# First mixer of a two-block transformer kernel: head projections with tokens on partitions, head norms along the free axis, then transposes

## The chip, the cores and the metric

The kernel runs as one program on one core of a Trainium2 chip. The metric is the device time of one execution in microseconds: 2159.94 us before the change, the median of three runs (2159.58 to 2167.09). TensorE multiplies a stationary operand (loaded by a weight load, up to 128x128) by a moving operand (up to 512 columns) into PSUM, in which a bank holds 512 fp32 values on each of 128 partitions. VectorE (DVE), ScalarE (ACT) and GpSimd (POOL) work beside it, and SyncE (SP) issues the DMAs.

## The reference, cut to what matters

Two transformer blocks on 512 tokens of width 1024, in fp32. The change lies in the mixer of the first block, between its two feed-forward parts:

```python
u = rms_norm(h, g_mix) @ w_in                       # 1024 -> 1952
q_lat, kv_lat, k_rope, qd, kd, vd = split(u, [256, 128, 32, 512, 512, 512])
# latent attention: 8 heads
q  = (rms_norm(q_lat, g_q_lat) @ w_q_up).reshape(S, 8, 96)     # 64 plain + 32 rotated
kv = (rms_norm(kv_lat, g_kv_lat) @ w_kv_up).reshape(S, 8, 128) # 64 keys + 64 values
q_nope = rms_norm(q[..., :64], g_q[:64]);  q_rot = apply_rope(rms_norm(q[..., 64:], g_q[64:]), cos, sin)
k_nope = rms_norm(kv[..., :64], g_k[:64]); k_rot = apply_rope(rms_norm(k_rope, g_k[64:]), cos, sin)
# differential attention: 4 heads, each with 2 x 64 queries and keys and 128 values
q = rms_norm(qd.reshape(S, 4, 2, 64), g_q);  k = rms_norm(kd.reshape(S, 4, 2, 64), g_k)
a = softmax(q1 @ k1.T * scale + bias) - lam * softmax(q2 @ k2.T * scale + bias)
o = rms_norm(a @ v, g_sub) * (1 - lambda_init)
h = h + concat(o_mla, o_diff) @ w_out
```

`rms_norm(x, g)` is x times the reciprocal root of the mean square of x along the last axis (plus 1e-6), times g. It is taken here over the 64 or 32 values of one head and one token.

## The kernel before, in words

Activations lie transposed: features on partitions, 512 tokens along the free axis. An fp32 product is made of three fp32r matmuls (`mm3`, L399 to L401): each operand is split into a rounded part (hi, by ScalarE) and a rest (lo, by VectorE or GpSimd), and hi·hi, hi·lo and lo·hi are added in PSUM. A weight block of 512 KB comes by a DMA into `wraw` (three buffers, L374), is split by ScalarE (L376) and by VectorE (L379) or GpSimd (L383) into `whl` (three buffers), and is then the stationary operand of 24 matmuls of 512 columns.

In the mixer a *task* is one weight block and what is done with it. `proj` (L615) multiplies a block of 128 output features with all tokens into one bank; `evacuate` (L630) multiplies it on VectorE by the token norm, which lies along the free axis as a tile broadcast over the partitions (`bcast`: four TensorE transposes and a ScalarE copy). There are twelve such blocks for the four differential heads (a query, a key and a value block each), four for the latents and the rotated key, and 72 matmuls of the up-projections in four tasks `t_mla`.

Since a head's 64 values lie across partitions, its mean square is a product with a matrix of ones: `row_rstd` (L483 to L489) squares a tile on ScalarE and multiplies it with a two-column constant on TensorE, four fp32 matmuls of two columns a tile, each of which shows as two records. The reciprocal roots then have tokens on partitions; `pairs` (L460) spreads them on VectorE and `bc2` (L468) transposes them, four transposes a tile, so that one VectorE operation (L769, L861, L869) can multiply them in. Values are needed with tokens on partitions: `transposes` (L564, L565) turns each value tile by four transposes and a ScalarE copy.

A generator `attention` goes through the items d0 to d3 and m0 to m3: scores, softmax, the transposes of the weights (L1076), the product with the values (L812, L911). `merge` interleaves it with the stream of tasks in a fixed ratio (100:135 by costs that the code yields), and the list `TASKS1` sets the order of the tasks. `need` holds an item back until its task is done and a lag has passed. From this program order, raised priorities (`high_priority`) and estimated times a scheduler writes the fixed order of each engine's queue. `stream` loads the weight of the running task and that of the next.

Of the kernel before, what the change touches and what calls it, by code (L numbers as in the profile page):

```python
# [31 lines left out]
TASKS1 = "q1 k1 v1 v0 kv q2 k2 v2 ql0 ql1 rq q3 bq k3 ple0 rkv kr v3 wkv bkv m0 m1 ple1 m2 wo2 m3 wo3 wo0"  # L32
# [47 lines left out]
def layout(inp):  # L80
# [20 lines left out]
    cols = []  # L101
    for h in range(HD):
        cols += [oqd + h * P + ar(P), okd + h * P + ar(P), ovd + h * P + ar(P)]
    cols += [oq + ar(256), okv + ar(128), kr, krp, kr, krp]
    L["w_inA"] = _a(w_in, np.concatenate(cols))
# [9 lines left out]
    wq = _a(g["w_q_up"][0], np.concatenate(qcols))  # L115
    L["w_qup"] = np.ascontiguousarray(wq.reshape(2, 4, P, 256).transpose(0, 2, 1, 3).reshape(2, P, 1024))
# [32 lines left out]
    L["c_rt1"] = np.concatenate([c, ss, c, ss], axis=0)  # L149
# [87 lines left out]
class Prog:  # L237
# [329 lines left out]
    def block1(self):  # L567
# [18 lines left out]
        rtab = self.U("rtab")  # L586
        nc.sync.dma_start(rtab, I["c_rt1"])
# [26 lines left out]
        def proj(w, evac=None, src=None, kc=KC, o=0):  # L614
            ps = self.G()  # L615
            for k in range(kc):
                c = slice(o + k * P, o + k * P + P)
                x = (xs if src is None else src)[k]
                self.mm3(ps, w[:, 0, c], w[:, 1, c], x[:, 0, :], x[:, 1, :], k == 0, k == kc - 1)
                if k % 2:  # L620
                    yield 1.3
            if evac is None and "rb" not in L_:
                L_["first"] = ps
                return
            evacuate(ps, L_["rb"] if evac is None else evac)
# [14 lines left out]
        def t_first(w):  # L640
            yield from proj(w)
            L_["r"] = self.rstd(acc2, D, "mix")

        def t_second(w):
            ps, first = self.G(), L_.pop("first")
            self.gemm(ps, w, xs, KC)
            L_["rb"] = self.bcast(L_.pop("r"), "mix")
            evacuate(first, L_["rb"])
            Y_[0] = [L_["y"]]
            evacuate(ps, L_["rb"])  # L650
            Y_[0].append(L_["y"])
            stats(("qk", 0), [(y, 0) for y in Y_[0]])
            yield

        def t_q(w, h):
            yield from proj(w)
            Y_[h] = [L_["y"]]

        def t_k(w, h):
            yield from proj(w)  # L660
            Y_[h].append(L_["y"])
            stats(("qk", h), [(y, 0) for y in Y_[h]])
            yield 1.0

        def t_v(w, h):
            yield from proj(w)
            vd[h] = self.U("vd")
            self.transposes(vd[h], L_["y"])
            mark(("v", h), 1.0)
            yield 0.4  # L670
# [32 lines left out]
        def t_b(w, k):  # L703
            L_["rb" + k] = self.bcast(L_["r" + k], k)
            yield 0.4

        def t_mla(w, p):
            if p % 2 == 0:
                L_["wq"] = w
            ql = [L_["ql", 0], L_["ql", 1]]  # L710
            ys = []
            for e in range(2):
                yield from proj(L_["wq"], L_["rbq"], ql, 2, ((2 * p + e) % 4) * 256)
                ys.append(L_["y"])
            for o in (0, 512):
                yield from proj(L_["wkv"], L_["rbkv"], [L_["kvl"]], 1, o + p * P)
                ys.append(L_["y"])
            yield 1.3
            vd["m", p] = self.U("vm")
            self.transposes(vd["m", p], ys[3])  # L720
            Y_["m", p] = ys
            stats(("m", p), [(ys[0], 1), (ys[1], 2), (ys[2], 0)])
            for e in range(2):
                rr = slice(64 * (1 - e), 64 * (1 - e) + 64)
                nc.vector.tensor_tensor(ys[e][rr], ys[e][rr], rtab[rr], op=OP.mult)
            yield 2.0
# [35 lines left out]

        def diff_n(h):
            yield from need(("qk", h))
            r = L_["qk", h]
            es = [self.pairs(r, 4, o) for o in (0, 2)]
            for y, e, g, d, n in ((Y_[h][0], es[0], gd[:, h : h + 1], q_, "dq"), (Y_[h][1], es[1], self.g1[:, GDK : GDK + 1], k_, "dk")):
# [5 lines left out]
            del Y_[h]  # L773
# [31 lines left out]
        def diff_o(h):  # L805
# [3 lines left out]
            for j in range(4):  # L809
                at = self.U("at")  # L810
                self.cols(at, a, j)
                mm(po, vd[h][:, j * P : (j + 1) * P], at, start=j == 0, stop=j == 3)  # L812
# [25 lines left out]
        def mla_kr(_):  # L838
# [4 lines left out]
            nc.vector.tensor_tensor(t, t, rtab, op=OP.mult)  # L843
# [12 lines left out]
        def mla_n(p):  # L856
            yield from need(("m", p))
            ys, r = Y_.pop(("m", p)), L_["m", p]
            es = [self.pairs(r, 6, o) for o in (4, 0, 2)]
            kn = self.U("kn")  # L860
            nc.vector.scalar_tensor_tensor(kn, ys[2], self.g1[:, GMKN : GMKN + 1], self.bc2(es[0]), op0=OP.mult, op1=OP.mult)  # L861
            yield 0.4
            q_["m", p], k_["m", p] = [], []
# [1316 lines left out]
```

## Time and profile before

| | before |
|---|---|
| time, median of three runs | 2159.94 us |
| the profiled execution, own time | 2162.42 us |
| its span, first to last instruction | 2160.6 us |
| TensorE busy | 97% of the span |
| VectorE, ScalarE, GpSimd busy | 44%, 33%, 25% |
| mean granted TensorE clock | 0.989 |
| the first mixer | about 380 to 712 us of the span |

How to read it: a busy TensorE is a queue that always has a matmul in flight. The recorded length of a matmul contains the passage through the array, so consecutive matmuls overlap in the records, and what one costs is the distance between the starts of neighbours. A granted clock of 1.00 is 2.4 GHz, 0.50 is 1.2 GHz.

### The profile page before, as it was taken

Reading aid. Unit: us, or ns where it says so; the run is one execution under the profiler, and the core shown is the slowest. Engines: PE = TensorE matmul, PEld = TensorE weight load, DVE = VectorE, ACT = ScalarE, POOL = GpSimd, SP = SyncE. Lnnn points to the kernel's source line nnn. Section 1 sums busy time; section 2 is a strip of 40 time slices with the busy share of each in tenths; the row PEclk is TensorE's granted clock in tenths of the full one; section 3 lists DMA queues with packets and bytes.
Section 4 is the critical chain, followed back from the end, with each engine's and each line's share of the span. In section 5 each row is a group of like instructions: output and inputs, shape, how many; then the busy total and the mean of one; then the engine's idle time right before and its main releaser. Section 6 shows DMA issues by size and latency. Waiting matters only on the chain.

```text
span 2160.6 us, 25910 instructions
## 1 busy us (share of the span) xinstructions
PE 2101.9 (97%) x10233; PEld 1508.2 (70%) x10233; DVE 955.3 (44%) x1695; ACT 720.2 (33%) x1201; POOL 547.1 (25%) x449
## 2 busy tenths in 40 slices
PE   8999999999999999999998999999999999999997
PEld 6888888767676788888777777667887455544544
DVE  4323234466775432323476994553353232322322
ACT  4213224445554422322444667442231111111112
POOL 3323234323331532323443445111230000000000
PEclk9999999999899999999999999999999999999999
DMA  4332323311010233332422111012626899999993
GB/s 163 98 90 96 98 89 116 115 59 59 10 50 30 88 98 95 92 97 88 124 78 69 50 40 45 30 49 69 241 78 234 355 412 411 421 411 414 408 395 158
DMA packets 67838, 330.73 MB, mean 153 GB/s; under 512 B 7792, under 2 KB 8960, under 8 KB 43648
## 3 DMA queue, kind: packets, MB, share of 16 engines
q1 hardware_dynamic: 67136, 327.97, 41.5%
q8 instruction: 82, 1.34, 0.2%
q10 hardware_dynamic: 576, 1.05, 0.1%
q14 instruction: 44, 0.36, 0.0%
HBM read 326.90 MB, written 2.10 MB: 152 GB/s over the span
## 4 chain that ended last, share of the span: by engine, by line
PE 83%; DVE 7%; ACT 4%; issue 3%; POOL 2%; DMA 0%; SPq 0%; DVEq 0%; POOLq 0%; ACTq 0%
PE pss L1743 10%; PE psg L399 10%; PE psg L401 10%; PE psg L400 10%; PE psg L1743 8%; PE pss L399 4%; PE pss L401 4%; PE pss L400 4%; PE pst L400 4%; PE pst L399 4%; PE pst L401 4%; PE pst L1743 4%; PE pst L486 1%; ACT whl L376 1%; PE pst L1748 1%
## 5 line engine op out<-in xcount | busy, mean ns | idle before, releaser
L383 POOL TENSOR_TENSOR whl<-wraw,whl 128x512 fp32r<-128x512 f32 x228 | 306.3, 1364 | 606.8 <-ACT whl L376 375.3
L376 ACT ACTIVATE whl<-wraw 128x1024 fp32r<-128x1024 f32 (+1 forms) x227 | 237.3, 1046 | 627.0 <-PE psg L401 254.5
L379 DVE TENSOR_TENSOR whl<-wraw,whl 128x1024 fp32r<-128x1024 f32 (+1 forms) x113 | 157.2, 1391 | 60.7 <-ACT whl L376 60.5
L2043 POOL TENSOR_TENSOR fr<-fv,mhalf 128x1 f32<-128x1 f32 x4 | 2.2, 547 | 513.8 <-DVE fv L2042 512.1
L1743 PE MATMUL pss<-mw,xe 128*64 128x512 f32 x512 | 115.3, 592 | 0.0
L1743 PE MATMUL pss<-mw,hT 128*64 128x512 f32 x480 | 109.7, 611 | 0.5 <-ACT hT L1921 0.5
L524 POOL TENSOR_TENSOR t<-t,t 128x512 f32<-128x512 f32 x44 | 57.3, 1303 | 202.4 <-DVE t L523 196.9
L1743 PE MATMUL psg<-mw,xe 128*64 128x512 f32 x480 | 108.1, 592 | 0.0
L523 DVE TENSOR_TENSOR t<-pss,rb_f 128x512 f32<-128x512 f32 x44 | 30.4, 691 | 163.1 <-PE pss L401 163.1
L556 DVE SCALAR_TENSOR_TENSOR h<-pst,h 128x512 f32<-128x512 f32 x48 | 33.2, 692 | 138.8 <-PE pst L401 138.8
L2016 DVE TENSOR_TENSOR h<-h,psg 128x512 f32<-128x512 f32 x120 | 81.2, 686 | 22.8 <-PE psg L1743 22.8
L1903 DVE SCALAR_TENSOR_TENSOR mt<-pss,sc,mt 128x512 f32<-128x512 f32 x16 | 12.0, 751 | 179.1 <-PE pss L1743 178.5
L1743 PEld LDWEIGHTS pss<-mw,xe 128*64 128x64 f32 x512 | 36.8, 137 | 73.1 <-issue 73.1
L1743 PEld LDWEIGHTS psg<-mw,xe 128*64 128x64 f32 x480 | 34.4, 137 | 68.1 <-issue 65.3
L1743 PEld LDWEIGHTS pss<-mw,hT 128*64 128x64 f32 x480 | 33.9, 140 | 65.1 <-issue 61.4
L395 DVE SCALAR_TENSOR_TENSOR yel<-pss,sc,yeh 128x512 fp32r<-128x512 f32 x32 | 24.0, 751 | 121.5 <-ACT yeh L394 121.5
L1743 PE MATMUL pst<-disp,uhh 128*128 128x256 f32 x256 | 66.7, 286 | 1.2 <-DVE disp L1821 1.2
L521 DVE TENSOR_TENSOR t<-psg,rb_f 128x512 f32<-128x512 f32 x44 | 30.4, 691 | 81.8 <-PE psg L401 76.2
L1743 PE MATMUL pst<-disp,uhl 128*128 128x256 f32 x256 | 65.2, 281 | 0.0
L1902 ACT ACTIVATE mt<-psg,sc 128x512 f32<-128x512 f32 x16 | 11.0, 688 | 157.1 <-PE psg L1743 134.2
L394 ACT ACTIVATE yeh<-pss,sc 128x512 fp32r<-128x512 f32 x32 | 22.0, 688 | 115.1 <-PE pss L1743 104.9
L433 POOL TENSOR_TENSOR acc<-acc,sq 128x512 f32<-128x512 f32 x33 | 49.7, 1506 | 39.1 <-ACT sq L432 36.8
(887 smaller groups left out, 5615.5 us busy)
## 6 DMA issues: line engine op xcount, KB each, us to landing
mw<-in_w SPq DMA_DIRECT2D x188, 1024.0 KB, 9.7
wraw<-in_w_gu SPq DMA_DIRECT2D x87, 512.0 KB, 3.6
wraw<-in_w_d SPq DMA_DIRECT2D x48, 512.0 KB, 3.6
wraw<-in_w2A SPq DMA_DIRECT2D x38, 512.0 KB, 3.6
wraw<-in_w_inA SPq DMA_DIRECT2D x16, 512.0 KB, 3.6
wraw<-in_w_out SPq DMA_DIRECT2D x8, 512.0 KB, 3.5
wraw<-in_w_pg SPq DMA_DIRECT2D x8, 512.0 KB, 3.6
wraw<-in_w_up SPq DMA_DIRECT2D x8, 512.0 KB, 3.7
```

The lines of the kernel that those rows point to most:

```text
L376: nc.scalar.activation(hl[:, 0, :n], raw[:, :n], AF.Copy)
L379: nc.vector.tensor_sub(hl[:, 1, :n], raw[:, :n], hl[:, 0, :n].bitcast(F32))
L383: nc.gpsimd.tensor_sub(hl[:, 1, c], raw[:, c], hl[:, 0, c].bitcast(F32))
L399: mm(ps, whi, xhi, start=first, stop=False)
L400: mm(ps, whi, xlo, start=False, stop=False)
L401: mm(ps, wlo, xhi, start=False, stop=last)
L433: (eng or nc.gpsimd).tensor_add(acc, acc, t)
L521: nc.vector.tensor_tensor(t1, pg, rb, op=OP.mult)
L524: nc.gpsimd.tensor_tensor(t2, t1, t2, op=OP.mult)
L556: nc.vector.scalar_tensor_tensor(self.h[m], py, 0.5, self.h[m], op0=OP.mult, op1=OP.add)
L1743: return self.next_to(nc.tensor.matmul(*args, **kw))
L2016: self.nc.vector.tensor_tensor(self.h[m], self.h[m], ps, op=OP.add)
```

## The change

The differential heads' queries, keys and values are projected with the tokens on partitions: the activations are the stationary operand and the weights the moving one, 256 columns wide (query and key of one head, or the values of two heads). One PSUM bank holds two tiles of 128 tokens. A block of 256 columns has two weights of 512 KB (the lower and the upper half of the 1024 inputs), and runs in four steps: lower half for bank 0, upper half for bank 0, upper half for bank 1, lower half for bank 1; so the first weight is held until the third of three tasks. ScalarE moves a bank to SBUF with the token's norm as a scale for each partition (two operations of 256 columns). The up-projections of the latents go the same way, with 512 moving columns: two tasks for queries, one for keys, one for values.

The mean squares are taken along the free axis: a square on ScalarE, a reduction on VectorE (`squares`), then a multiplication by the reciprocal root on VectorE (`scaled`). Only after that are queries and keys turned (`turned`: four transposes), and gain, split, or gain and rotation are applied out of PSUM. Values need no transposes. The statistics matmuls, `pairs` and `bc2` of these tiles, the transposes of values and the broadcasts of the two latent norms go. The table of the rotation becomes two, with ones for the plain part (a second DMA of 256 KB). The token norm of the first block is computed after the first 24 matmuls of 256 columns.

```diff
-TASKS1 = "q1 k1 v1 v0 kv q2 k2 v2 ql0 ql1 rq q3 bq k3 ple0 rkv kr v3 wkv bkv m0 m1 ple1 m2 wo2 m3 wo3 wo0"
+TASKS1 = "qk1 v0 kv qk2 v1 ql0 ql1 rq qk3 ple0 rkv kr wkv mk mq0 mv ple1 mq1 wo2 wo3 wo0"
...
-        nc.sync.dma_start(rtab, I["c_rt1"])
+        rtab = [self.U("rtab") for e in range(2)]
+        for e in range(2):
+            nc.sync.dma_start(rtab[e], I["c_rt1"][e])
...
-        def t_k(w, h):
-            yield from proj(w)
-            Y_[h].append(L_["y"])
-            stats(("qk", h), [(y, 0) for y in Y_[h]])
-            yield 1.0
-
-        def t_v(w, h):
-            yield from proj(w)
-            vd[h] = self.U("vd")
-            self.transposes(vd[h], L_["y"])
...
+        def t_block(w, steps, then):
+            for b, s in steps:
+                if b not in L_:
+                    L_[b] = self.G()
+                for i in (2 * b, 2 * b + 1):
+                    ps = L_[b][:, (i % 2) * 256 : (i % 2) * 256 + 256]
+                    tk = slice(i * P, i * P + P)
+                    for k in range(4):
+                        c = slice(k * 256, k * 256 + 256)
+                        x = xs[4 * s + k]
+                        first, last = s == b and i % 2 + k == 0, s != b and i % 2 == 1 and k == 3
+                        mm(ps, x[:, 0, tk], w[:, 0, c], start=first, stop=False)
+                        mm(ps, x[:, 1, tk], w[:, 0, c], start=False, stop=False)
+                        mm(ps, x[:, 0, tk], w[:, 1, c], start=False, stop=last)
+                    yield 1.4
+                if s != b:
+                    then(b, L_.pop(b))
+
+        def squares(src, ms):
+            sq = self.U("sq")
+            with self.tc.high_priority(offset=HP1):
+                nc.scalar.activation(sq, src, AF.Square)
+                nc.vector.tensor_reduce(ms, sq.rearrange("p (s f) -> p s f", f=64), axis=AX.X, op=OP.add)
+
+        def scaled(out, src, r):
+            with self.tc.high_priority(offset=HP1):
+                nc.vector.tensor_tensor(out.rearrange("p (s f) -> p s f", f=64), src.rearrange("p (s f) -> p s f", f=64),
+                                        r.unsqueeze(2).to_broadcast([P, 8, 64]), op=OP.mult)
+
+        def evac(t, b, ps):
+            with self.tc.high_priority(offset=HP1):
+                for i in (0, 1):
+                    c = slice(256 * i, 256 * i + 256)
+                    nc.scalar.activation(t[:, c], ps[:, c], AF.Copy, scale=rx[0][:, 2 * b + i : 2 * b + i + 1])
...
+            return [(wB[2 * i], one), (wB[2 * i + 1], lambda w1: t_block(w1, [(0, 1), (1, 1)], then)),
+                    (None, lambda _: t_block(w.pop(), [(1, 0)], then))]
...
+        def t_up(w, lat, o, key, then):
+            ys = []
+            for i in range(4):
+                ps = self.G()
+                tk = slice(i * P, i * P + P)
+                for k, x in enumerate(lat):
+                    c = slice(o + k * 512, o + k * 512 + 512)
+                    self.mm3(ps, x[:, 0, tk], x[:, 1, tk], w[:, 0, c], w[:, 1, c], k == 0, k == len(lat) - 1)
+                y = self.U("vm" if then is None else "ym")
+                with self.tc.high_priority(offset=HP1):
+                    nc.scalar.activation(y, ps, AF.Copy, scale=L_[key][:, i : i + 1])
...
+                    squares(y, v[:, 8 * i : 8 * i + 8])
...
+            for i, y in enumerate(ys):
+                scaled(y, y, r[:, 8 * i : 8 * i + 8])
...
+        def turned(ys, o, w):
+            ps = self.PT()
+            n = 512 // w
+            for i in range(4):
+                c = (i % n) * w + o
+                nc.tensor.transpose(ps[:, i * P : i * P + P], ys[i // n][:, c : c + P], self.ident)
+            return ps
...
         def diff_n(h):
-            es = [self.pairs(r, 4, o) for o in (0, 2)]
...
-                t = self.U("dn")
-                nc.vector.scalar_tensor_tensor(t, y, g, self.bc2(e), op0=OP.mult, op1=OP.mult)
                 d[h] = self.HL(n)
-                self.split(d[h], t, lo=nc.gpsimd)
+                self.split(d[h], turned(ys, o, 256), scale=g)
...
         def mla_n(p):
-            nc.vector.scalar_tensor_tensor(kn, ys[2], self.g1[:, GMKN : GMKN + 1], self.bc2(es[0]), op0=OP.mult, op1=OP.mult)
+            nc.scalar.activation(kn, turned(Y_["mk"], p * P, 512), AF.Copy, scale=self.g1[:, GMKN : GMKN + 1])
...
     def stream(self, tasks):
             load(i + 1)
+            if ap is None and i + 1 < len(tasks) and i + 1 in ws:
+                load(i + 2)
```

## Rows read from the trace of the kernel before

**Rows 1.** The page: busy us (share of the span) xinstructions

```profile
PE 2101.9 (97%) x10233; PEld 1508.2 (70%) x10233; DVE 955.3 (44%) x1695; ACT 720.2 (33%) x1201; POOL 547.1 (25%) x449
```

**Rows 2.** Stretches of the mixer: busy us by engine, granted clock, DMA share, GB/s

```profile
382.00:712.00 330.00, 315.95 (x1574) 233.04 (x1573) 207.59 (x453) 166.79 (x331) 101.38 (x78) 0.97 0.17 54
...
541.50:555.20 13.70, 12.14 (x51) 9.80 (x51) 8.88 (x27) 6.77 (x15) 6.30 (x5) 0.50 0.00 1
...
630.00:634.00 4.00, 4.00 (x14) 3.27 (x15) 1.83 (x6) 0.45 (x2) 0.84 (x1) 0.57 0.52 156
```

**Rows 3.** The chain of waits in the mixer, by line

```profile
by line: PE psg L399 14.0%; PE psg L401 13.9%; PE psg L400 13.7%; PE pst L486 6.0%; PE psg L911 4.6%; PE pst L1076 4.3%; PE psg L812 2.8%; ACT sb L792 2.7%; issue 2.6%; PE pss L414 2.5%; PE pss L399 2.3%; PE pst L468 2.1%; DVE sb L788 2.1%;
```

**Rows 4.** Timeline, TensorE, 512 moving columns: start us, length; nine starts apart

```profile
388.23 0.40 PE L401 MATMUL psg<-xs2h,whl 128*128 128x512 f32 x1
...
390.32 0.40 PE L401 MATMUL psg<-xs5h,whl 128*128 128x512 f32 x1
```

**Rows 5.** Timeline, TensorE, 256 moving columns: twenty starts apart

```profile
1645.06 0.28 PE L1743 MATMUL pst<-disp,uhh 128*128 128x256 f32 x1
...
1647.42 0.28 PE L1743 MATMUL pst<-disp,uhh 128*128 128x256 f32 x1
```

**Rows 6.** The tile of that product: its weight loads, ns min/median/max

```profile
L1743 PEld LDWEIGHTS pst<-disp,uhh x256: 186/188/193, 1643.9 to 2070.2; 128*128 128x128 f32 x128
```

**Rows 7.** TensorE groups of the mixer: xcount, busy us, mean ns, idle before

```profile
L486 PE MATMUL pst<-cb,sq 128*128 128x2 f32 x168 | 22.2, 258 | 0.4 <-DVE rv L489 0.4
...
L564 PE MATMUL pst<-ident,y 128*128 128x128 f32 x32 | 5.1, 281 | 0.3 <-DVE y L630 0.2
...
L454 PE MATMUL pst<-ident,r_q 128*128 128x128 f32 x4 | 0.6, 285 | 1.7 <-POOL r_q L447 1.7
```

**Rows 8.** Timeline, TensorE, up to the fall of the granted clock

```profile
537.81 0.95 PE L486 MATMUL pst<-cb,sq 128*128 128x2 f32 x8
538.62 0.63 PE L564 MATMUL pst<-ident,y 128*128 128x128 f32 x4
539.09 1.84 PE L486 MATMUL pst<-cb,sq 128*128 128x2 f32 x16
541.30 5.04 PE L486 MATMUL pst<-cb,sq 128*128 128x2 f32 x24 [0.37 <-DVE rv L489]
```

**Rows 9.** VectorE groups of the mixer

```profile
L887 DVE TENSOR_REDUCE mn<-pss 128x1 f32<-128x512 f32 x32 | 21.4, 685 | 14.4 <-PE pss L401 14.4
...
L630 DVE TENSOR_TENSOR y<-psg,rb_mix 128x512 f32<-128x512 f32 x16 | 10.8, 687 | 14.2 <-PE psg L401 14.1
L460 DVE COPY bce<-rr 128x512 f32<-128x512 f32 x21 | 8.1, 421 | 0.1
L725 DVE TENSOR_TENSOR y<-y,rtab 64x512 f32<-64x512 f32 x8 | 8.0, 995 | 0.4 <-ACT sq L483 0.2
...
L861 DVE SCALAR_TENSOR_TENSOR kn<-y,g,pst 128x512 f32<-128x512 f32 x4 | 3.0, 744 | 0.4 <-PE pst L468 0.4
...
L843 DVE TENSOR_TENSOR krn<-krn,rtab 128x512 f32<-128x512 f32 x1 | 0.7, 691 | 0.0
```

**Rows 10.** ScalarE groups of the whole span

```profile
L394 ACT ACTIVATE yeh<-pss,sc 128x512 fp32r<-128x512 f32 x32 | 22.0, 688 | 115.1 <-PE pss L1743 104.9 <-PE pss L1929 10.2
...
L483 ACT ACTIVATE sq<-y 128x512 f32<-128x512 f32 x21 | 12.8, 625 | 4.1 <-DVE y L630 4.0
...
L391 ACT ACTIVATE khh<-psg 128x264 fp32r<-128x264 f32 x8 | 3.1, 386 | 3.9 <-PE psg L1239 3.9
...
L565 ACT COPY vd<-pst 128x512 f32<-128x512 f32 x4 | 2.3, 583 | 4.2 <-PE pst L564 4.2
```

**Rows 11.** Waits in the mixer: us in total, times, longest

```profile
ACT whl L376 <- PE psg L401: 36.5, 15, 4.9
```

**Rows 12.** Timeline, GpSimd, the last sum for the token norm

```profile
382.60 1.80 POOL L433 TENSOR_TENSOR acc<-acc,sq 128x512 f32<-128x512 f32 x1 [1.21 <-ACT sq L432]
```

**Rows 13.** Timeline, TensorE, the mixer's first matmul

```profile
379.93 0.39 PE L399 MATMUL psg<-xs0h,whl 128*128 128x512 f32 x1
```

More of the change, by code (lines that the diff above doesn't have):

```diff
@@ L100, in layout @@
     krp = okr + np.concatenate([ar(16, 32), ar(16)])
[L101 to L105, printed above, removed]
+    L["w_inA"] = _a(w_in, np.concatenate([oq + ar(256), okv + ar(128), kr, krp, kr, krp]))
+    blocks = [np.concatenate([o + h * P + ar(P) for o in (oqd, okd)]) for h in range(HD)] + [ovd + v * 256 + ar(256) for v in range(2)]
+    L["w_inB"] = np.concatenate([w_in[:, c].reshape(2, 4, P, 256).transpose(0, 2, 1, 3).reshape(2, P, 1024) for c in blocks])
     qcols = []
@@ new lines, in values, with then, block, one @@
+        def values(v):
+            def then(b, ps):
+                t = self.U("vd")
+                evac(t, b, ps)
+                for h in (2 * v, 2 * v + 1):
+                    for i in (0, 1):
+                        vd[h, 2 * b + i] = t[:, 256 * i + P * (h % 2) : 256 * i + P * (h % 2) + P]
+                    mark(("v", h), 1.0)
+            return then
+        rx = []
+        def block(i, then, norm=None):
+            w = []
+            def one(w0):
+                w.append(w0)
+                yield from t_block(w0, [(0, 0)], then)
+                if norm is not None:
+                    norm()
+            return [(wB[2 * i], one), (wB[2 * i + 1], lambda w1: t_block(w1, [(0, 1), (1, 1)], then)),
+                    (None, lambda _: t_block(w.pop(), [(1, 0)], then))]
@@ L672, in t_ql, with norm @@
+        def norm():
+            rx.append(self.rstd(acc2, D, "mix"))
+            L_["rb"] = self.bcast(rx[0], "mix")
         def t_ql(w, c):
@@ L701, in t_r @@
             yield 0.5
[L703 to L710, printed above, removed]
-            ys = []
[L712 to L726, printed above, removed]
+        def t_up(w, lat, o, key, then):
+            ys = []
+            for i in range(4):
[5 more added lines that the diff above has]
+                y = self.U("vm" if then is None else "ym")
+                with self.tc.high_priority(offset=HP1):
+                    nc.scalar.activation(y, ps, AF.Copy, scale=L_[key][:, i : i + 1])
+                ys.append(y)
+                yield 0.7 * len(lat)
+                if then is not None:
+                    if i == 0:
+                        v = self.S("ms", 32)
+                    squares(y, v[:, 8 * i : 8 * i + 8])
+            if then is None:
+                vd["m"] = ys
+                return
+            r = self.S("rr", 32)
+            with self.tc.high_priority(offset=HP1):
+                nc.vector.tensor_scalar(v, v, 1.0 / 64, EPS, op0=OP.mult, op1=OP.add)
+                self.rsqrt(r, v)
+            for i, y in enumerate(ys):
+                scaled(y, y, r[:, 8 * i : 8 * i + 8])
+            Y_[then] = ys
+            mark(then, LAG)
```

92 lines of the change are left out of this document (48 added, 44 removed).

## Prediction

> **What bounds the kernel now.** The page's busy table comes first: TensorE is busy for 97% of the span, no other engine for half of it [rows 1]. The change touches only the first mixer, so the same table by stretches comes next: in its 330 us TensorE is busy for 315.95, VectorE for 207.59 (63%), ScalarE for 166.79 (51%) and GpSimd for 101.38 (31%) [rows 2]. The chain of waits in this stretch runs mostly over TensorE's own queue, and one line of it is small work: the statistics matmuls of L486 hold 6.0% of the chain, some 20 us of 330 [rows 3]. So the mixer costs what TensorE's instructions cost, one start after another, plus 14 us without a matmul, plus 17 us in which the granted clock was lower [rows 2]. A change is priced by the distances between starts that it takes out or puts in, then by the clock, then by the waits.
>
> **Projections.** 288 matmuls of 512 columns (twelve blocks of 24) become 576 of 256 (six blocks of 96). 512 columns: nine starts in 2.09 us, 0.232 each [rows 4]. 256 columns with a 128x128 load before every one, fp32r on both sides: twenty starts in 2.36 us, 0.118 each [rows 5]. 576 x 0.118 - 288 x 0.232 = 68.0 - 66.8 = **+1.2 us**. From the two sides: the four-transpose distance below (0.11) would make it -3.4; a weight load in its full recorded length of 0.188 [rows 6] would make it +41.5. I take 0.118: same shapes, same type, same alternation, 256 records of that group.
>
> The up-projections keep 72 matmuls of 512 columns: 0.
>
> One rule speaks against this edit. The rows show a load of 0.188 us recorded before each matmul, and starts 0.118 apart: load and matmul overlap on full 128-row operands [rows 5, 6]. The Trainium skill, TensorE: Matmul & The Clock Gate, section Part 3, "The mechanism", says that a weight load overlaps matmuls in flight only where it goes to another row group; the same page gives 107 ns for loading 128 columns, so an estimate from its figures would be 0.118 + 0.107 per matmul, and the sum of this edit +62. The trace does not agree with it, and it stays as a rival of small chance.
>
> **Statistics.** Twenty tiles (eight of the differential heads, twelve of the latent heads) times eight records of two columns leave, 160 of 168; the rotated key keeps eight [rows 7]. Sixteen records lasted 1.84 us and eight 0.95, so 0.111 each [rows 8]: **-17.8 us**. TensorE executes nothing in their place: the reduction goes to VectorE.
>
> **Transposes.** Eight value tiles no longer turn: 32 transposes [rows 7]. Four last 0.63 us with 0.28 for one alone [rows 7, 8], so 0.11 to 0.12 apart: -3.6. The two latent broadcasts are eight more: -0.9. `turned` issues as many (80) as `bc2` did for the same tiles: 0. Together **-4.5 us**.
>
> **The clock.** From 541.5 to 555.2 the granted clock was at its lower level, 1.2 GHz, and for 3.4 us after 630 again [rows 2]. The first fall came when TensorE had issued statistics in three bursts, 8, 16 and the start of 24, with four transposes between and 0.37 us idle at most [rows 8]. 12.14 busy us at half speed are worth at most 6.1 lost, the second stretch 1.7: between 0 and -7.8. Since these bursts leave the program I take **-6**. The Trainium skill, same page, Part 1, says that idle time lets the clock fall; in the rows before the fall TensorE was hardly idle but did matmuls of two columns. By idleness alone the fall need not go with the statistics, and the sum is 6 smaller: the first rival.
>
> **The other engines.** VectorE loses 28 evacuations of 0.687, twenty copies of 0.421, eight rotations of 0.995 and four `kn` of 0.744: 38.6 us. It gains twenty reductions and twenty multiplications [rows 9]. No reduction out of SBUF to eight values stands in the trace; the one of 512 PSUM values takes 0.685, the multiplication of two SBUF tiles 0.691 in one row and 0.995 in another: 27.5 to 33.6. Net -5 to -11. ScalarE gains 24 evacuations of 256 columns (0.386 for 264) and twenty of 512 with a scale (0.688), loses ten copies of 0.583 [rows 10]: +17 us, 51% to some 59% of the stretch. Eight lo splits go from GpSimd to VectorE, where they take the place of eight `dn` of the same kind. None of it is the longest queue, so 0 on the sum; its latency is in the waits.
>
> **Waits.** The broadcast of the query-latent norm, with its 1.7 us of idle TensorE, goes [rows 7]. New ones, each an estimate from rows:
> - The token norm is now needed after 24 x 0.118 = 2.8 us from the mixer's first matmul at 379.93, at 382.8 [rows 13]; the last sum on GpSimd ends at 384.4 [rows 12]. If its matmuls stand there in the queue, 1.6 us.
> - For the keys a tile has three matmuls, 0.7 us, while ScalarE needs 0.69 for the evacuation and 0.63 for the square: 4 x 0.6 = 2.4 us with nothing between, 0 where attention fills it.
> - The second weight of a block can be split only when the other's last reader before it is through. This block's last step and the next one's first hide it (48 x 0.118 = 5.7 us); if that cover is thin, 1 us for each of five blocks.
> - The extra 256 KB table goes on SP's queue behind the first weights of the mixer and is read long after: 0.
>
> I take +4 net, between -2 and +9.
>
> **Sum.** +1.2 - 17.8 - 4.5 - 6 + 4 = -23.1. Span 2160.6, and 1.8 around it: 2162.4 - 23 = 2139 for the profiled execution; this lies 2.5 above the median of the runs, so **2137** there.
>
> **The rivals.**
> - *The clock falls all the same.* For it: TensorE was also without a matmul for 1.56 of those 13.7 us [rows 2], and short transposes stay. Against it: no two-column burst is left but one of eight. 2137 + 6 = 2143.
> - *The statistics were filler.* More than half of what leaves (12 latent tiles, 96 records, 10.7 us, and 16 value transposes, 1.8 us) stood beside attention items whose softmax sits on VectorE and ScalarE; if attention's own chain sets the end there, these 12.5 us turn into idle TensorE: 2137 + 12.5 = 2149.5. For it: VectorE is at 63% in the mixer against 44% over the span [rows 1, 2]. Against it: the idle total is only 14 us of 330 now.
> - *Slower: evacuations behind weights.* ScalarE's queue is in order, and its weight splits already wait for a matmul to free `whl` 15 times, 36.5 us, 2.4 each [rows 11]. Today VectorE evacuates and is not held up. After the change 12 banks and 16 up-projection tiles are evacuated behind such a split, with three banks to run ahead. Each exposure costs 2.4 us, and from ten of 28 on the gain of 23 is gone; 14 give 2137 + 34 = 2171, all 28 give 2204. Against it: the scheduler places splits by the same estimated times, and the banks of a block are 5.7 us apart.
> - *Weight loads exposed*: 0.188 in place of 0.118 for 576 matmuls, +40: 2177. Against it: [rows 5].
>
> **How the numbers follow.** Forecast 0.55, clock 0.16, filler 0.16, evacuations 0.10, loads 0.03. A measurement here can tell about 0.5% (10.8 us) from no change, so faster means below 2149.1, slower above 2170.7. Forecast and clock lie below, and half of the filler case: 0.55 + 0.16 + 0.08 = 0.79 faster. Slower are the loads and half of the evacuations, 0.08; the other halves, 0.13, are the same. The range reaches down to no new waits, the whole 7.8 of the clock and nine of today's 14 idle us (2137 - 4 - 1.8 - 9 = 2122), and up to the filler case with the waits at their bound (2149.5 + 5 = 2154).
>
> **What would show it.** Right: no L486 but eight records; starts 0.118 apart in the 256-column groups; the mixer some 23 us shorter and the other stretches the same; a clock of 1.00 through it; VectorE's busy time down by 5 to 11 in it and ScalarE's up by 17. Wrong: idle TensorE in front of an evacuating bank, with ScalarE's evacuation or weight split as releaser (the evacuations), or in front of `cols` and the value products (filler); distances near 0.19 (loads); a half clock again (the first rival).

## The result and the profile after

The changed kernel takes 2177.35 us, median of five runs (2174.27 to 2178.93), beside 2159.94 for the kernel before on the same chip (2158.56 to 2167.09): ratio 1.0072, 95% interval 1.0061 to 1.0083. It is slower by 17.4 us; the forecast was 2137, faster.

The profiled execution spans 2175.2 us, 14.6 more than before; the other 2.8 lie mostly in the profiled execution of before, which was 2.5 above its median. Between the last matmul of the first feed-forward part and the last one of the output projection lie 338.1 us in place of 326.2: the mixer, +11.9. The second feed-forward part stayed at 370 us; the next block's stages ahead of the experts went from 567.6 to 570.2.

The page, busy time by engine, answers to [rows 1]:

```profile
PE 2095.9 (96%) x10321; PEld 1512.8 (70%) x10321; DVE 951.4 (44%) x1671; ACT 734.1 (34%) x1233; POOL 537.4 (25%) x441
```

The mixer of the changed kernel, and stretches of it, with the columns of [rows 2]. Both first windows begin at 382 and end 6 us behind the mixer's last matmul:

```profile
382.00:724.00 342.00, 305.09 (x1651) 232.32 (x1650) 203.33 (x429) 181.15 (x363) 91.14 (x70) 0.94 0.17 53
505.00:521.20 16.20, 13.35 (x66) 7.86 (x63) 12.74 (x39) 6.82 (x17) 3.75 (x3) 1.00 0.15 42
521.20:538.30 17.10, 14.85 (x44) 10.14 (x41) 7.46 (x23) 9.48 (x21) 0.20 (x1) 0.52 0.06 23
538.30:555.40 17.10, 13.47 (x59) 10.02 (x57) 7.94 (x15) 13.97 (x24) 5.40 (x5) 0.99 0.21 62
555.40:572.50 17.10, 8.24 (x27) 5.65 (x27) 12.03 (x16) 7.59 (x15) 13.05 (x10) 0.51 0.00 0
```

TensorE is busy 10.9 us less than in [rows 2], and the window is 12 us longer: idle TensorE went from 14.05 to 36.91 us, and the granted clock from 0.97 to 0.94 (44.4 us at 1.2 GHz in the trace's clock records, 17.1 before). VectorE's busy time is 4.3 lower, ScalarE's 14.4 higher. In the mixer of the kernel before, no 17.1 us have less than 13.8 us of TensorE.

The 256-column projections, twenty starts apart, beside [rows 5]:

```profile
387.41 0.28 PE L652 MATMUL psg<-whl,xs7l 128*128 128x256 f32 x1
...
389.78 0.28 PE L651 MATMUL psg<-whl,xs6h 128*128 128x256 f32 x1
```

2.37 us, 0.118 each. The groups that answer to [rows 7], [rows 9] and [rows 10], first TensorE, then VectorE, then ScalarE:

```profile
L836 PE MATMUL pst<-ident,ym 128*128 128x128 f32 x48 | 9.5, 340 | 8.2 <-DVE ym L668 7.1 <-ACT kn L931 0.8 <-ACT rbh L988 0.3
...
L486 PE MATMUL pst<-cb,sq 128*128 128x2 f32 x8 | 1.7, 335 | 0.0
```

```profile
L663 DVE TENSOR_REDUCE ms<-sq 128x8 f32<-128x512 f32 x20 | 13.7, 684 | 25.5 <-ACT sq L662 25.5
L668 DVE TENSOR_TENSOR ym<-ym,rr 128x512 f32<-128x512 f32 x12 | 9.6, 863 | 0.1
```

```profile
L675 ACT ACTIVATE y<-psg,r_mix 128x256 f32<-128x256 f32 x16 | 6.7, 469 | 22.6 <-PE psg L653 22.6
```

Statistics are down to eight records, and where ScalarE evacuates the queries and keys of the differential heads, it has waited for TensorE (22.6 us), not TensorE for it. What TensorE waits for ahead of the first latent scores (us in total, times, longest), changed kernel:

```profile
PE pst L836 <- DVE ym L668: 7.1, 2, 4.4
PE pss L414 <- DVE mn L860: 4.7, 5, 2.4
PE psg L399 <- ACT pp L808: 4.3, 1, 4.3
PE pst L442 <- POOL accq L433: 3.2, 1, 3.2
```

The tiles are `ym`, the scaled latent queries; `mn`, the row minima of the differential heads' scores, nearly all of d3's; `pp`, a bank of a `ple` task, which the change leaves alone and ScalarE moves out; and `accq`, the sum for the query-latent norm. The largest such wait of before was 1.7 [rows 7]. The timeline of the worst place, ScalarE, VectorE and TensorE together (start, length, engine and line, wait):

```profile
520.84 0.50 PE L414 MATMUL pss<-dkh,dqh 64*128 64x512 f32 x1 [2.41 <-DVE mn L860]
...
550.89 0.69 ACT L931 ACTIVATE kn<-pst,g 128x512 f32<-128x512 f32 x1
...
554.87 0.63 ACT L391 ACTIVATE kth<-krs 64x512 fp32r<-64x512 f32 x1
555.40 0.61 ACT L662 ACTIVATE sq<-ym 128x512 f32<-128x512 f32 x1
555.92 0.56 ACT L808 COPY pp<-psg 128x512 f32<-128x512 f32 x1
556.05 0.69 DVE L663 TENSOR_REDUCE ms<-sq 128x8 f32<-128x512 f32 x1 [8.05 <-ACT sq L662]
...
556.53 0.79 PE L399 MATMUL psg<-pTh,whl 128*128 128x512 f32 x1 [4.35 <-ACT pp L808]
...
563.14 4.64 DVE L668 TENSOR_TENSOR ym<-ym,rr 128x512 f32<-128x512 f32 x4
...
563.89 0.69 PE L836 MATMUL pst<-ident,ym 128*128 128x128 f32 x2 [4.43 <-DVE ym L668]
...
569.94 0.68 DVE L860 CUSTOM_DVE_ANT_0 sb<-pss,dist 128x512 f32<-128x512 f32 x1
...
571.32 0.79 PE L414 MATMUL pss<-dkh,dqh 64*128 64x512 f32 x1
```

The head norm of the first latent queries runs here: the last of its four squares (555.40) stands on ScalarE behind the key's evacuation and splits (550.89 to 555.5), then come reduction, root and scaling (563.14), then the turned transposes. d3, which attention's program order has behind them, had its first scores issued at 520.84 (counted from d2's, which begin at 504.65); VectorE takes their row minima only at 569.94, behind the scaling and the rotated queries, and d3's second scores follow at 571.32. Between these steps TensorE ran only six matmuls of a `ple` task and eight transposes of d2's weights.

### The profile page after: what moved, and what is told of

Same layout as the page of the kernel before. It is cut to its first block, busy times and chain, and to the rows that moved or that the text cites. A ratio compares the mean times of both kernels' runs of the same rounds, so it can differ in the third digit from the quotient of the medians.

```text
span 2175.2 us, 26066 instructions
## 1 busy us (share of the span) xinstructions
PE 2095.9 (96%) x10321; PEld 1512.8 (70%) x10321; DVE 951.4 (44%) x1671; ACT 734.1 (34%) x1233; POOL 537.4 (25%) x441
## 4 chain that ended last, share of the span: by engine, by line
PE 81%; DVE 8%; ACT 4%; issue 4%; POOL 3%; DMA 0%; SPq 0%; DVEq 0%; ACTq 0%; POOLq 0%
PE pss L1820 10%; PE psg L399 9%; PE psg L400 8%; PE psg L401 8%; PE psg L1820 8%; PE pss L399 4%; PE pss L401 4%; PE pss L400 4%; PE pst L400 4%; PE pst L401 4%; PE pst L399 4%; PE pst L1820 4%; ACT whl L376 1%; PE psg L651 1%; PE psg L653 1%
## 5 line engine op out<-in xcount | busy, mean ns | idle before, releaser
L2093 DVE TENSOR_TENSOR h<-h,psg 128x512 f32<-128x512 f32 x120 | 81.2, 686 | 22.6 <-PE psg L1820 22.6
```

The source lines that it names most:

```text
L2093: self.nc.vector.tensor_tensor(self.h[m], self.h[m], ps, op=OP.add)
```

## Experiments

"Mixer" is the length given above; "m0" the first latent head, "d3" the last differential head. Times are medians of 4 to 10 executions, ratios stand against the kernel before, run beside it. The mixer is read from one profiled execution, whose own time can differ from the median: b_v3_early 5.2 us below it, a_fill 6.1, a_m0late 4.0 and o_plelate 4.3 above, v1_late 3.7 and vl_ratio115 4.2 below, the others up to 3.3. After the table each group has its edit (`...` marks lines left out), the expectation on record and the finding.

| kernel | us | ratio, 95% interval | mixer |
|---|---|---|---|
| before / after | 2159.9 / 2177.4 | 1.0072 [1.0061, 1.0083] | 326.2 / 338.1 |
| b_nostat | 7228 | not comparable | 312.1 |
| diff_only | 2172.5 | 1.0057 [1.0040, 1.0075] | 337.3 |
| mla_only | 2161.0 | 0.9996 [0.9984, 1.0007] | 320.8 |
| evac_dve | 2178.4 | 1.0087 [1.0064, 1.0111] | 339.6 |
| chain_hp | 2177.5 | 1.0064 [1.0042, 1.0086] | 340.5 |
| v1_late | 2166.0 | 1.0020 [1.0010, 1.0030] | 327.2 |
| v1_last | 2160.4 | 0.9995 [0.9985, 1.0004] | 322.6 |
| b_v3_early | 2181.1 | 1.0094 [1.0077, 1.0111] | 338.3 |
| o_plelate | 2157.0 | 0.9977 [0.9968, 0.9987] | 324.0 |
| o_mk | 2160.0 | 0.9992 [0.9982, 1.0001] | 321.9 |
| vl_ratio115 | 2158.2 | 0.9986 [0.9976, 0.9996] | 319.4 |
| v1_last_hp | 2158.1 | 0.9980 [0.9969, 0.9992] | 322.5 |
| a_m0late | 2179.8 | 1.0073 [1.0047, 1.0098] | 341.7 |
| b_m0late | 2165.5 | 1.0014 [1.0004, 1.0023] | 330.3 |
| p_m0late | 2158.7 | 0.9987 [0.9977, 0.9996] | 322.0 |
| l115_m0late | 2161.4 | 1.0000 [0.9990, 1.0010] | 322.4 |
| a_fill | 2198.3 | 1.0164 [1.0148, 1.0181] | 365.9 |
| v_fill | 2180.2 | 1.0092 [1.0074, 1.0109] | 345.1 |

**1. Were the statistics on the path of the kernel before?** The kernel before without its 160 records; it leaves out the mean squares (roots are taken of squared values), so the experts' load is another one and only the mixer can be read.

```diff
-        ps = self.PT()
+        ps = self.PT() if items[0][1] == 3 else None
...
-            for i in range(4):
+            if kind == 3:
+              for i in range(4):
...
-        nc.vector.tensor_scalar(v, ps[:, : 4 * w], EPS, None, op0=OP.add)
+        nc.vector.tensor_scalar(v, ps[:, : 4 * w] if kind == 3 else sq[:, : 4 * w], EPS, None, op0=OP.add)
```

> The kernel before with the statistics matmuls of the head norms left out (160 of the 168 two-column records; the reciprocal roots are taken of squares instead of mean squares, the rotated key keeps its own). Theory 'filler' (the work taken out only filled time in which attention's softmax chain sets the end): it stays within 8 us of before, 2152 to 2160. Theory 'path' (every start distance on TensorE counts in the kernel before, as the prediction had it, and the loss of the changed kernel is something new): 17.8 us of statistics and 4 to 6 us of half clock go, 2135 to 2142.

The mixer's window, to be set beside the first of [rows 2]:

```profile
382.00:698.00 316.00, 293.81 (x1415) 211.62 (x1414) 212.85 (x453) 166.01 (x332) 101.15 (x78) 0.98 0.18 57
```

14 us shorter. TensorE is busy 22 us less, and 8 of these turned into idle. So most of the statistics was on the path, as the prediction had it, but not all. The time at 1.2 GHz in the mixer fell from 17.1 to 10.2 us: the records alone account for less than half of it.

**2. Which half of the change loses?** One part alone: the differential heads (with the changed kernel's early value task), or the latent heads.

```diff
 # diff_only, order of tasks
+TASKS1 = "qk1 v0 kv qk2 v1 ql0 ql1 rq bq qk3 ple0 rkv kr wkv bkv m0 m1 ple1 m2 wo2 m3 wo3 wo0"
 # mla_only, order of tasks
+TASKS1 = "q1 k1 v1 v0 kv q2 k2 v2 ql0 ql1 rq q3 k3 ple0 rkv kr v3 wkv mk mq0 mv ple1 mq1 wo2 wo3 wo0"
```

> The change for the differential heads alone (blocks of 256 columns, evacuation on ScalarE, norms along the free axis, turned); latent heads, their statistics and their tasks as before. Theory 'late chain of the latent queries' (the loss is that m0's transposes stand in TensorE's queue ahead of d3's scores and wait for a chain of square, reduction, root and scaling that ScalarE runs late): faster than before, by 64 statistics records and 16 transposes (9 us), 2145 to 2155. Theory 'evacuation on ScalarE': slower or the same, 2160 to 2175, since 24 of the 40 evacuations are still there. Theory 'attention pacing' (tasks that got shorter no longer cover attention): about half the loss, 2165 to 2170.

> The change for the latent heads alone; differential heads as before. Theory 'late chain of the latent queries': the whole loss and more, since the gain of the differential heads is missing: 2175 to 2190. Theory 'evacuation on ScalarE': 16 of 40 evacuations, 2160 to 2170. Theory 'attention pacing': about half the loss, 2165 to 2170.

The differential part with the early value task brings +11.1 of the mixer's +11.9. The latent part alone, with the values at their old places, shortens the mixer by 5.4 and lengthens the next block's stages ahead of the experts by 4.5, total unchanged. So the latent queries' chain is not the main cause. Both totals lie where 'evacuation on ScalarE' put them; the next run speaks against that theory.

**3. Is ScalarE's queue the place?** All 40 evacuations to VectorE; or the chain of the head norms 400 in place of 60 ahead in the planner's order.

```diff
 # evac_dve (the up-projections' likewise)
-                    nc.scalar.activation(t[:, c], ps[:, c], AF.Copy, scale=rx[0][:, 2 * b + i : 2 * b + i + 1])
+                    nc.vector.tensor_scalar(t[:, c], ps[:, c], rx[0][:, 2 * b + i : 2 * b + i + 1], None, op0=OP.mult)
 # chain_hp
-HP1, HP2 = 60, 30
+HP1, HP2 = 400, 30
```

> The changed kernel with its 40 evacuations on VectorE (one multiplication by the token's norm out of PSUM) in place of ScalarE. Theory 'evacuation on ScalarE' (banks and chains wait behind weight splits and other work on ScalarE): most of the loss comes back, 2140 to 2160. Theory 'late chain of the latent queries': the squares and the two steps of the root stay on ScalarE behind the key splits, so the wait stays: 2168 to 2182.

> The changed kernel with the priority offset of evacuations, squares, roots and scalings raised from 60 to 400, so that the scheduler places them ahead of splits and copies that come earlier in the program. Theory 'late chain of the latent queries' (7.1 us of waits for the scaled queries, 4.35 for a bank behind key splits on ScalarE, and the half clock after them): 2160 to 2168. Theory 'attention uncovered': 2170 to 2180, since d2's scores stay alone.

Both stay within 1.1 us of the changed kernel. Who evacuates does not set the time. chain_hp says less than it was meant to: in its trace TensorE's waits for `ym` (7.1 us) and `pp` (4.3) are those of the changed kernel, and the last square still starts behind the key splits. The priority did not move it, so no run shows what an earlier chain would be worth.

**4. Is it the order of the tasks?** The change came with its own order: values two heads at a time, both blocks ahead of the latent queries (`v0 ... v1 ql0 ql1`), where the kernel before has `v3` behind `kr`.

```diff
 # v1_late, v1_last: the changed kernel
-"qk1 v0 kv qk2 v1 ql0 ql1 rq qk3 ple0 rkv kr wkv mk mq0 mv ple1 mq1 wo2 wo3 wo0"
+"qk1 v0 kv qk2 ql0 ql1 rq qk3 v1 ple0 rkv kr wkv mk mq0 mv ple1 mq1 wo2 wo3 wo0"
+"qk1 v0 kv qk2 ql0 ql1 rq qk3 ple0 rkv kr v1 wkv mk mq0 mv ple1 mq1 wo2 wo3 wo0"
 # b_v3_early: the kernel before
-"q1 k1 v1 v0 kv q2 k2 v2 ql0 ql1 rq q3 bq k3 ple0 rkv kr v3 wkv bkv m0 m1 ple1 m2 wo2 m3 wo3 wo0"
+"q1 k1 v1 v0 kv q2 k2 v2 v3 ql0 ql1 rq q3 bq k3 ple0 rkv kr wkv bkv m0 m1 ple1 m2 wo2 m3 wo3 wo0"
```

> The changed kernel with one task moved in TASKS1: the value block of heads 2 and 3 (v1) goes from before the latent queries to behind qk3. Theory 'attention uncovered' (values now come two heads at a time and early, so the projections are used up before d2's and d3's scores, which then wait for their own softmax with nothing else in TensorE's queue; the kernel before had q3, k3 and v3 left there): d2's scores are covered again, the idle of 505 to 530 us and the half clock after it shrink, 2155 to 2168. Theory 'late chain of the latent queries': nothing moves there, 2172 to 2182.

> The same with v1 behind the rotated key, where v3 stood before. Theory 'attention uncovered': 96 matmuls (11 us) of cover stand beside d2 and the way to d3, 2148 to 2165, at least as good as behind qk3. Theory 'late chain of the latent queries': 2172 to 2182.

> The kernel before, with nothing changed but the place of one task: the value block of head 3 goes from behind the rotated key to before the latent queries, as values stand in the changed kernel. Theory 'attention uncovered': the kernel before loses 4 to 12 us, 2164 to 2172, with idle TensorE and half clock beside d2 and d3. Any theory that puts the loss on the new instructions (evacuation, chains, statistics along the free axis): within 3 us of before.

One value task placed later gives the changed kernel back 17.0 us. One placed earlier costs the kernel before 20.1 against the runs beside it, more than the 4 to 12 expected; its profiled execution is the shortest of four, and there the mixer is 12.1 longer. The task moved holds 96 matmuls of 256 columns in the first case (two heads), 24 of 512 and four transposes in the second (one head). The mixer's windows cut where m0's first score starts, columns as in [rows 2]; first the kernel before, then the changed one, then v1_last, then b_v3_early:

```profile
382.00:562.50 180.50, 174.95 (x869) 132.45 (x868) 104.53 (x274) 86.32 (x167) 56.52 (x45) 0.96 0.22 69
562.50:712.00 149.50, 141.00 (x707) 100.58 (x706) 103.06 (x179) 80.47 (x165) 44.86 (x33) 0.99 0.11 36
```

```profile
382.00:580.80 198.80, 173.09 (x1021) 140.28 (x1020) 110.29 (x267) 103.87 (x204) 54.77 (x42) 0.91 0.22 69
580.80:724.00 143.20, 132.01 (x634) 92.05 (x631) 93.04 (x163) 77.28 (x160) 36.37 (x28) 0.98 0.10 30
```

```profile
382.00:565.50 183.50, 168.76 (x1025) 137.41 (x1023) 112.82 (x269) 104.00 (x205) 56.48 (x42) 0.94 0.24 76
565.50:709.00 143.50, 131.40 (x631) 91.93 (x631) 93.57 (x161) 77.04 (x160) 36.34 (x28) 0.98 0.10 30
```

```profile
382.00:576.50 194.50, 178.57 (x869) 134.24 (x868) 105.73 (x274) 86.57 (x169) 57.75 (x45) 0.96 0.20 64
576.50:724.00 147.50, 139.43 (x706) 99.43 (x707) 102.86 (x179) 80.18 (x164) 44.69 (x33) 1.00 0.12 36
```

Behind m0's first score the change wins 6.3 us. Ahead of it it loses 18.3: idle TensorE is 25.7 there against 5.6. The changed kernel and v1_last do the same work ahead of m0 (1021 and 1025 records seen); with v1 moved, idle falls from 25.7 to 14.7, the time at 1.2 GHz from 37.5 to 20.5, and busy time with it by 4.3. The task is not out of the way, it stands where TensorE had nothing, and d2's first exponential comes 13.7 us earlier into the mixer.

**5. Can the rest be had by order, pacing or priority?** All on v1_last.

```diff
 # o_plelate; o_mk (a value task's mark only when its second block is out)
+"qk1 v0 kv qk2 ql0 ql1 rq qk3 rkv kr wkv mk v1 mq0 ple0 mv ple1 mq1 wo2 wo3 wo0"
+"qk1 v0 kv qk2 ql0 ql1 rkv wkv rq qk3 mk kr v1 mq0 ple0 mv ple1 mq1 wo2 wo3 wo0"
 # vl_ratio115
-        self.merge(attention(), self.stream(tasks), 100.0, 135.0)
+        self.merge(attention(), self.stream(tasks), 100.0, 115.0)
 # v1_last_hp
+HP1, HP2 = 400, 30
```

> The changed kernel with its last value task directly behind the first half of the latent up-projection (mk) and the first ple task behind mq0 (a value task's mark is set when both of its blocks are out). With the last value task behind kr the mixer took 322.6 us (326.2 in the kernel before) and PE still waited 6.8 us in three waits for ym, which the latent queries' chain writes. 'Cover': what the task list has behind mq0 decides these waits; with ple0 there they fall below 3 us, and the total from 2160.4 to 2151-2157. 'Late chain': the chain itself is late because ScalarE and VectorE are busy with the differential heads; ym's waits stay at 5-8 us and the total at 2158-2163. A third way: the value task behind mk makes the value products of the third head late, and the time is lost there (2160-2166).

> As the kernel with ple0 behind mq0, and mk pulled ahead as well, before kr and the last value task: the latent keys' chain (copies, squares, turned transposes) is then done before d2 and d3 score. 'Cover': more of the work that waits for nobody stands where d2 and d3 score, 2148-2156. 'Late chain': the same copies and squares now stand in front of the differential heads' exponentials on ScalarE, attention is later, 2162-2170.

> The changed kernel with its last value task behind kr (2160.4 us, mixer 322.6) and attention issued faster against the tasks (weights 100 to 115 in place of 100 to 135), so that tasks last longer beside it. 'Cover': projections are left for more of the scores, idle PE in the mixer falls from 25.2 us to 15-20, total 2150-2157. If marks and not the weights hold attention back, nothing moves (within 0.3% of 2160.4). If attention's instructions are then ahead of the chains they need on ScalarE and VectorE, slower: 2165-2175.

> The changed kernel with its last value task behind kr (2160.4 us) and the chain of copies, squares and scalings of the head norms 400 instead of 60 ahead in the planner's order. 'Late chain': PE's waits for ym (10.5 us in four) are a matter of these instructions standing behind others in ScalarE's and VectorE's queues, they halve, and the total falls to 2152-2157. 'Cover': the priority does as little as it did in the changed kernel itself (2177.5 beside 2177.4), 2158-2163.

Each gains 0.4 to 3.4 us on v1_last, with overlapping intervals. o_plelate has the lowest median of the study and beats the kernel before and the changed one: 2157.0, 0.9977 [0.9968, 0.9987]. Its total is at the edge of what 'cover' gave; its waits for the scaled tiles, which 'cover' had below 3 us, fell from 6.8 us in v1_last to 3.5:

```profile
PE pst L837 <- DVE ym L668: 3.5, 4, 2.1
```

In v1_last_hp the priority again moved nothing: its mixer (322.5) and its wait for `ym` (6.8) are those of v1_last.

**6. Is m0's preparation ahead of d3's scores what holds the mixer?** Moved behind them, in the changed kernel (a), the kernel before (b), o_plelate (p) and vl_ratio115 with o_plelate's mark (l115).

```diff
-                if n + 2 < len(items):
-                    yield from ready(*items[n + 2])
+                for k in {2: (), 3: (4, 5)}.get(n, (n + 2,)):
+                    if k < len(items):
+                        yield from ready(*items[k])
```

> The changed kernel (2177.4 us, mixer 338.1) with the preparation of the first latent head (m0) behind the scores of the last differential head (d3) in place of ahead of them; nothing else moves. 'Chain ahead of d3': d3's exponentials begin 150 to 170 us into the mixer instead of 192, the mixer falls by 10 to 20 us and the total to 2157-2167. 'Order of the value tasks' alone: d3 begins earlier but its time is lost again at the latent heads, total 2172-2180. 'Clock': the half-clock stretches (44 us) stay and the total moves by less than 5 us.

> The kernel before (2159.9 us, mixer 326.2, d3's exponentials from 172 us) with the same move of m0's preparation behind d3's scores. If the kernel before is held by that chain too, d3 begins 10 to 20 us earlier and the total falls to 2148-2155. If its head norms on partitions were done in time, d3 moves by under 5 us and the total stays within 0.2% of 2160.

> The changed kernel with its last value task behind mk and the first ple task behind mq0 (2157.0 us, mixer 324.0, d3 from 167 us), and m0's preparation behind d3's scores. 'Chain ahead of d3': d3 from 150-160 us, mixer 308-316, total 2142-2150. If d3 is held by its own projections or by the value products of the third head: 2153-2160.

> The changed kernel with its last value task behind kr and attention issued at 100 to 115 (2158.2 us, mixer 319.4, d3 from 173 us), and m0's preparation behind d3's scores. 'Chain ahead of d3': d3 from 150-160 us, mixer 304-312, total 2140-2150. Otherwise 2153-2160.

All four missed their first theory: d3 came 26 to 40 us earlier in each and no total gained. Exponentials of d3 (L864) and m0 (L961) on ScalarE, first of each; the changed kernel, then a_m0late:

```profile
572.56 0.72 ACT L864 ACTIVATE sb<-sb,mn 128x512 f32<-128x512 f32 x1 [1.81 <-DVE mn L863]
...
593.97 0.67 ACT L961 ACTIVATE am<-pss,mn 128x512 f32<-128x512 f32 x1
```

```profile
533.55 0.72 ACT L864 ACTIVATE sb<-sb,mn 128x512 f32<-128x512 f32 x1 [0.89 <-DVE mn L863]
...
598.23 0.69 ACT L961 ACTIVATE am<-pss,mn 128x512 f32<-128x512 f32 x1
```

d3 came 39 us earlier and m0 4 us later: its preparation, pushed back, is now the late thing. What counts here is when m0 can start; which of the two waits for the other does not. m0's start alone does not decide across other orders: o_plelate's first exponential of m0 comes 7.8 us earlier into the mixer than v1_last's, and its mixer is 1.4 longer in the profiled executions.

**7. Is TensorE's work still on the path?** 160 short records on constants, used by nobody, one set behind each square of the head norms; in the changed kernel and in v1_last.

```diff
                 nc.vector.tensor_reduce(ms, sq.rearrange("p (s f) -> p s f", f=64), axis=AX.X, op=OP.add)
+            ps = self.PT()
+            for i in range(4):
+                nc.tensor.matmul(ps[:, 2 * i : 2 * i + 2], self.ident, self.cb1[:, 0:2], start=True, stop=True)
```

> The changed kernel (2177.4 us, mixer 338.1) with 80 matmuls of two columns on constants (160 records, the number that the change removed) issued one set of four behind each square of the head norms; their results are used by nobody. 'Work': TensorE's work is still on the path, the mixer is 14 to 18 us longer, total 2191-2197. 'Gaps': the 36.9 us of idle PE takes them, the mixer stays within 4 us, total 2174-2182. If they keep the clock up or replace waits: below 2174.

> The same 160 short matmuls in the kernel with its last value task behind kr (2160.4 us, mixer 322.6, idle 25.2 us). 'Work': mixer +14 to +18 us, total 2174-2178. 'Gaps': mixer within 5 us, total 2158-2165; then the saving of the change is hidden behind waits there, and what is left to gain goes by the chains and not by TensorE.

The records, and the part ahead of m0's first score (604.9), in a_fill:

```profile
L666 PE MATMUL pst<-cb,ident 128*128 128x2 f32 x160 | 25.6, 284 | 0.1
```

```profile
382.00:604.90 222.90, 199.95 (x1149) 166.65 (x1147) 109.94 (x269) 104.73 (x205) 54.76 (x42) 0.85 0.20 62
```

They cost 20.9 and 19.8 us in the medians, more than the 17.8 they were priced at, though 37 and 27 us of idle TensorE lie about: 'gaps' falls in both. In a_fill's profiled execution the part ahead of m0's first score grew from 198.8 to 222.9 us, with the granted clock down from 0.91 to 0.85. The records themselves start 0.111 us apart where the granted clock is 1.00 and 0.213 where it is 0.50, so the lower clock explains a price above 17.8. My reading of the rest, not shown by itself: the order of TensorE's queue is fixed, and work put ahead of a wait pushes the awaited chain back with it.

## Why the prediction was wrong

**The prices of TensorE's work held roughly,** and the other engines' nearly (VectorE -4.3 where -5 to -11 stood, ScalarE +14.4 for +17). 0.118 a start for 256 columns, and with it the rival "weight loads exposed" falls; 160 records gone, worth 14 us where they were taken out of the kernel before and 20 where put into the changed one (17.8 said, clock and idle included in both); behind m0's first score, 6.3 us won. The Trainium skill, TensorE: Matmul & The Clock Gate, Part 3, "The mechanism", has by the sentence that the prediction used each load exposed, while the same section also lets a load into the background weight buffer run ahead. The measured 0.118 speaks against the first and agrees with the second, for full 128-row operands.

**The step that failed is "Waits": "I take +4 net, between -2 and +9".** Idle TensorE in the mixer rose by 36.91 - 14.05 = 22.9 us, 20.2 of it ahead of m0's first score. I bounded new waits singly, by the evacuation or square that each adds, and never asked what the new order of tasks leaves in TensorE's queue when such a wait comes. Of the rows that I priced, the token norm has 1.7 after (1.6 said); the query-latent norm, whose 1.7 I took off, has 3.2, and that goes with the order (3.1 in b_v3_early, none in v1_last). The large ones are the scaled tiles 7.1, the differential scores 4.7 (0.2 of it at 419), and `pp` 4.3, at 520 to 581, where the projections had been used up: the last one of the block's input ends at 515. Part of the 7.1 is VectorE's: the four scalings that start at 563.14 take 4.64 us beside GpSimd's sums for the `ple` task, the four at 542.5, with GpSimd idle, 2.5.

**"The clock: -6" failed with it.** The records that I blamed are gone and the clock fell more often; b_nostat, in which nothing else went, still has 10.2 us at 1.2 GHz where 17.1 stood. The balance of the two first windows is +12.0 = -21.1 (+1.2 - 17.8 - 4.5) + 22.9 + clock, so the clock took 10.2; from its rows, half of the busy time at 1.2 GHz (an estimate), (14.85 + 8.24 + three stretches of 3.4)/2 = 16.6, less 7.8 before, is 8.8. The falls at 521.2 and 555.4 each follow a stretch with 2.9 and 3.6 us without a matmul. The Trainium skill, TensorE: Matmul & The Clock Gate, Part 1, has the clock fall through idleness. The trace agrees for these two falls. More short records went with more of it too: ahead of m0's first score, a_fill has 68.3 us at 1.2 GHz and the changed kernel 37.5, v_fill 37.5 and v1_last 20.5, with 2.8 and 2.9 us less idle TensorE.

**What each part cost is known only in part.** By medians b_v3_early stands 21.2 above the kernel before, diff_only 8.6 below b_v3_early, and the changed kernel 4.9 above diff_only; these steps add up to 17.5 by their making. The prediction's prices are nothing for the order, 1.2 - 7.1 - 3.6 = -9.5 for the differential heads and -10.7 - 0.9 - 1.7 = -13.3 for the latent ones. Each ratio is known to some 0.2%, 4 us. In the traces the mixer goes 326.2, 338.3, 337.3, 338.1: +12.1, -1.0, +0.8. So the order was left out, at 12 to 21 us. Whether the differential heads gave their 9.5 is open. That the latent heads, added at this order, did not give their 13.3 is clear by either count; at the old order (mla_only) they shorten the mixer by 5.4. Where the rest of it goes, I read from the waits above: into the chain of copy, square, reduction, root, scaling and transpose. No run has that chain earlier at the same order.

**The rivals.** "The clock falls all the same" came true and was too small. "The statistics were filler" saw idle TensorE coming, but at the latent heads, where 2.7 us came, and by a mechanism that a_fill speaks against; of it, b_nostat shows 8 us turned into idle and 14 won. "Evacuations behind weights" had the right sign and kind (a head-norm step is held up in ScalarE's queue) and the wrong holder and place: key splits at 551 to 555, which held a square and the bank of `pp`. Its own test, evac_dve, moved nothing.

**Open.** With the last value task at its old place (v1_last) the change is worth nothing, and in the best order tried (o_plelate) 3 to 5 us, where the forecast had 23; the order of the values explains some 17 of the 40 us between forecast and result, and the rest stays open. In v1_last idle TensorE ahead of m0 is 14.7 against 5.6; its two largest waits are for the latent heads' tiles:

```profile
PE pst L836 <- DVE ym L668: 6.8, 3, 3.2
PE psg L399 <- ACT ym L767: 3.7, 3, 2.7
```

Orders with the last value task behind mq0 were not tried, nor a kernel in which the latent queries' chain really runs earlier, so whether full cover or an earlier chain would bring the rest is open. So is why the stage some 360 us behind the mixer differs by up to 4.5 us between kernels whose code there is the same; the runs show only that its time at 1.2 GHz varies (6.8 us before, 17.1 after, 20.5 in mla_only).

## What to carry to other kernels

Where a list of tasks is woven with a latency-bound chain, price the order that comes with a change as a part of its own: find the instruction that starts the last long chain (here the first latent head's scores), and ask of each task whether it stands ahead of it where the engine is full or where the engine has nothing. Work taken off an engine whose queue has a fixed order is won only if no longer wait for another engine takes its place; idle time elsewhere in the stretch did not pay for added work here (a_fill, v_fill). A new norm chain on two other engines needs independent work queued between its producer and its consumer, and the task list is where that is decided.

## What the runs showed of the hardware

- Two-column fp32 matmul records, each with a 128x128 load, start 0.111 to 0.112 us apart at a granted clock of 1.00 and 0.213 to 0.214 at 0.50 (a_fill): about the 0.118 of a 256-column fp32r matmul at 1.00. 160 of them cost 19.8 to 20.9 us, part of them at the lower clock.
- The multiplication of a 512-column tile by eight scales a row, broadcast over 64 columns, took 0.68 to 0.69 us on VectorE in the 15 of 20 cases with no GpSimd instruction beside it, as two plain tiles do (0.691); four of the five beside one took 1.72 to 1.79 (the changed kernel). The means of 0.863 and 0.954 mix the two.
- The reduction of 512 SBUF values to eight took 0.684, that of 512 PSUM values to one 0.685.
- ScalarE's evacuation of 256 columns with a scale took 0.469 where 264 plain columns took 0.386.
